# The first transfers of a two-layer decoder trunk: two token tiles on ScalarE's queue, token tiles one piece ahead, a buffer of its own for the fourth unit of weights

## Chip, cores and metric

One core of one Trainium2 chip. The metric is device time in microseconds (us) of one execution, the median of three runs. Engines are called by what they do: TensorE (PE, with PEld for its weight loads) multiplies matrices, VectorE (DVE) and ScalarE (ACT) work elementwise, GpSimd (POOL) does small jobs, and SyncE (SP) issues most transfers from memory. The issuing queues are written SPq and ACTq. The data itself is moved by 16 DMA engines.

## What is computed

Two layers of a causal decoder on 256 tokens of width 2048, in float32. Layer 0 mixes tokens by a block-sparse attention (with 256 tokens only its own block counts, so it is plain causal attention of 16 heads of 128), layer 1 by a latent attention with low-rank queries and keys. Each layer ends with a gated channel mixer of width 5632.

```python
def reference(x, attn_norm, ffn_norm, ...):
    pos = jnp.arange(x.shape[1], dtype=jnp.int32)
    for i in range(DEPTH):
        m, j = i % N_MIXERS, i // N_MIXERS
        h = rms_norm(x, attn_norm[i])
        if m == 0:
            y = moba_attention(h, pos, moba_wq[j], moba_wk[j], moba_wv[j],
                               moba_gq[j], moba_gk[j], moba_wo[j])
        elif m == 1:
            y = mla_attention(h, pos, ...)
        ...
        x = x + y
        h = rms_norm(x, ffn_norm[i])
        x = x + conv_glu_ffn(h, ffn_w_gate[i], ffn_w_up[i], ffn_conv_w[i],
                             ffn_conv_b[i], ffn_w_down[i])
    return x
```

## The kernel before

The tokens lie transposed in one tile `xT`: 16 token tiles of 128 features by 256 tokens, 128 KB each, all in on-chip memory for the whole run. All weights pass by once as a stream (`Stream`, L54). The stream is cut into 370 units, mostly of 1 MB, each of mostly four pieces of 128 x 512 numbers (256 KB). A piece is read from its `raw` buffer and split into a high half `whi` (a cast, L104 on ScalarE; piece 0 alone on VectorE, L102) and a low half `wlo` (the rest, L105 on VectorE), so that TensorE can work at reduced width and add three products: high by high, low by high, high by low. The tokens are split the same way into the two halves of `h` (L279 on ScalarE, L284 on VectorE), after scaling by the gain of the norm; the division by the root mean square comes later, on the result.

The program is a list of quanta, one per piece. Nothing is reordered (`manual_schedule`): for each quantum `q` the last loop (L1049) first runs what was planned ahead of it, then splits pieces up to a few beyond `q` (`ws.split`, L1052; one ahead at first, one more for every six quanta, at most four), then the six products of the piece (`tok_major`, L229, for the first 192 pieces), then what was planned beside it. In the first 16 quanta (the queries of the first four heads) token tile `q` is scaled and split right before its piece, so on ScalarE the order is: high half of tile q, then the cast of the next piece.

Three `raw` buffers hold units (`AHEAD_UNITS = 3`). `split` asks for unit `u + 2` when it starts unit `u` (L96, `load` L66), and the load waits until the unit that had the buffer is split. The first three units, 12 pieces, come as single pieces from `begin` (L75), interleaved with the token tiles: `ends` gives for each piece up to which tile the tokens are asked for right behind it. All of these go out on SP's queue but the very first piece, which is on ScalarE's (L84). The parameters `par` of the norms go first of all. Weight unit 3, the rest of `par`, the rotary tables `tab` and the `gains` follow once the loop runs (`load_constants`, L183, in quantum 9).

The program has eight completion semaphores for these transfers, used in turn: a transfer is issued only when the eighth before it has landed. An issuing queue works strictly in order, so a transfer that waits holds up those behind it.

The attention pool `att` (L165) holds what the attention of layer 0 needs; the latent attention of layer 1 opens another (`att2`) and uses the same helpers. In it are scratch tiles: `junk` (L378) takes the squares that a reduction of VectorE produces on the way to its sums, `ro1` and `ro2` (L430) the two products of the rotation, `kvjunk` (L843) the squares of the latent keys. Each has two buffers, used in turn. `oT` in the same pool is the attention's result, read by TensorE in the output projection (`plan_wo`, L674).

Of the kernel before, what the change touches and what calls it, by code (L numbers as in the profile page):

```python
# [10 lines left out]
F32 = mybir.dt.float32  # L11
# [6 lines left out]
P = 128  # L18
# [24 lines left out]
AHEAD_UNITS = 3  # L43
# [10 lines left out]
class Stream:  # L54
# [17 lines left out]
            self.raw[u] = t  # L72
            self.loaded += 1

    def begin(self, load_x):  # L75

        ends = (2, 2, 3, 4, 6, 6, 8, 8, 10, 10, 13, 16)
        load_x(0, 1)
        at = 1
        for u in range(AHEAD_UNITS):  # L80
            src, k, n = self.units[u]
            self.raw[u] = t = self.raw_pool.tile([P, 4 * 512], F32, name="raw")
            for i in range(k):
                queue = self.nc.scalar if u == i == 0 else self.nc.sync  # L84
                queue.dma_start(t[:, i * n : (i + 1) * n], src[:, i * n : (i + 1) * n])
                end = ends[u * k + i]
                if end > at:
                    load_x(at, end)
                    at = end
        self.loaded = AHEAD_UNITS  # L90

    def split(self, upto):
        while self.split_to < min(upto, len(self.pieces)):
            i = self.split_to
            u, j, n = self.pieces[i]
            self.load(u + AHEAD_UNITS)  # L96
            w = self.raw[u][:, j * n : (j + 1) * n]
            b, c = self.starts(u, j)
            hi = self.part_pool.tile([P, 512 + ROOM], F32R, name="whi")[:, b : b + 512]
            lo = self.part_pool.tile([P, 512 + ROOM], F32R, name="wlo")[:, c : c + 512]  # L100
            if i == 0:
                self.nc.vector.tensor_copy(hi[:, :n], w)  # L102
            else:
                self.nc.scalar.copy(hi[:, :n], w)  # L104
            self.nc.vector.tensor_tensor(  # L105
                lo[:, :n], w, hi[:, :n].bitcast(F32), op=ALU.subtract
            )
            self.parts[i] = (hi, lo, n)
            self.split_to += 1
# [6 lines left out]
def trunk(ctx: ExitStack, tc: tile.TileContext, a, out):  # L116
    nc = tc.nc
# [43 lines left out]
    ws = Stream(nc, raw_pool, part_pool, units, starts)  # L161
# [3 lines left out]
    att_pool = att.enter_context(tc.tile_pool(name="att", bufs=2))  # L165
    xT = keep.tile([P, KD, S], F32, name="xT")
# [9 lines left out]
    warm = const.tile([P, 1], F32, name="warm")  # L176
    nc.scalar.activation(warm, ones, AF.Square)
    nc.sync.dma_start(par[:, :C_CW], a["par"][:, :C_CW])
    ws.begin(lambda j0, j1: nc.sync.dma_start(xT[:, j0:j1, :], a["xT"][:, j0:j1, :]))
    tab = const.tile([P, T_END], F32, name="tab")  # L180
    gains = const.tile([P, G_END], F32, name="gains")

# [170 lines left out]
    class Heads:  # L353
# [21 lines left out]

        def squares(self, t):
            for i in range(self.n):
                junk = att_pool.tile([P, P], F32, name="junk", bufs=2)  # L378
                nc.vector.tensor_tensor_reduce(  # L379
                    out=junk[:, : self.dh], in0=self.x[:, t, i], in1=self.x[:, t, i], scale=1.0,  # L380
                    scalar=0.0, op0=ALU.mult, op1=ALU.add, accum_out=self.ss[:, t, i : i + 1],
                )
# [34 lines left out]
        def rotate(self, t, stages=(0, 1)):  # L417
            if not self.rot:
                return
            n, rot = self.n, self.rot  # L420
            hf = rot // 2
            tb, C, Sn = self.tabs
            ct = tb[:, C + t * rot : C + (t + 1) * rot]
            st = tb[:, Sn + t * rot : Sn + (t + 1) * rot]
            x = self.x[:, t]
            def over(s):
                return s[:, None, :].to_broadcast([P, n, s.shape[1]])

            def part(name):
                r = att_pool.tile([P, 16 * 32], F32, name=name, bufs=2)  # L430
                return r[:, : n * rot].rearrange("p (n r) -> p n r", n=n)

            if 0 in stages:
                t1, t2 = self.rot_parts = part("ro1"), part("ro2")
                nc.vector.tensor_tensor(t1, x[:, :, :rot], over(ct), op=ALU.mult)
                nc.vector.tensor_tensor(t2[:, :, :hf], x[:, :, hf:rot], over(st[:, :hf]), op=ALU.mult)
            if 1 in stages:
                t1, t2 = self.rot_parts
                nc.vector.tensor_tensor(t2[:, :, hf:], x[:, :, :hf], over(st[:, hf:]), op=ALU.mult)
                nc.vector.tensor_tensor(x[:, :, :rot], t1, t2, op=ALU.add)  # L440
# [398 lines left out]
    def kva_stats():  # L839
        ss = small.tile([P, NT, 2], F32, name="kvss")  # L840
        for t in range(NT):
            for k, (lo, hi) in enumerate(((0, 512), (512, 576))):
                junk = att_pool.tile([P, 512], F32, name="kvjunk", tag="ro1", bufs=2)  # L843
                nc.vector.tensor_tensor_reduce(
                    out=junk[:, : hi - lo], in0=env["ckv"][:, t, lo:hi], in1=env["ckv"][:, t, lo:hi],
                    scale=1.0 / (hi - lo), scalar=0.0, op0=ALU.mult, op1=ALU.add,
                    accum_out=ss[:, t, k : k + 1],
                )
        ms = small.tile([P, NT * 2], F32, name="kvms")
        nc.vector.tensor_scalar(ms, ss.rearrange("p t k -> p (t k)"), EPS, None, op0=ALU.add)  # L850
        env["kvr"] = small.tile([P, NT * 2], F32, name="kvr")
        nc.gpsimd.tensor_tensor(env["kvr"], ms, mhalf[:, : NT * 2], op=ALU.pow)
# [144 lines left out]

    at(q, open_room)
    at(q, kva_stats)
    at(q + 3, kva_scale)  # L1000
    at(q + 7, kva_rotate)
# [166 lines left out]
```

## Time and profile before

| | us |
|---|---|
| runs shown: median (lowest, highest) | 2099.79 (2099.7, 2100.92) |
| profiled execution: its own time | 2099.88 |
| its span, first to last instruction | 2098.0 |
| TensorE busy in the span | 2089.0 |
| VectorE busy | 1405.3 |
| ScalarE busy | 1138.3 |
| bytes moved | 391.83 MB |

The profile is of one execution. Times inside it count from the start of its span. A row of a timeline gives the start, the length, the engine, the line of the kernel, the operation and its tiles (written from what is read), and in brackets the idle time before it and what ended that. A row of a transfer gives the tile, the queue and the median time from issue to landing. Products follow each other more closely than their lengths say: they are pipelined, so the distance of two starts is the measure of their rate.

### The profile page before, as it was taken

What the parts mean: (1) busy time and instruction counts of PE and PEld (TensorE: products, weight loads), DVE (VectorE), ACT (ScalarE), POOL (GpSimd) and SP (SyncE); (2) the same over time, 40 slices, a digit from 0 to 9 for tenths busy, and PEclk for the clock granted to TensorE, in tenths of its full rate; (3) what the DMA queues carried; (4) which work ended last, traced back from release to release, by engine and by line L of the source; (5) the groups of instructions that cost most, each with busy time, mean ns of one, the idle gap of its engine ahead of it and who ended that gap; (6) DMA issues with size and microseconds to landing.
All of it is one profiled execution on the core that took longest, in us unless ns stands there. A gap on an engine that the chain in (4) does not pass through costs nothing.

```text
span 2098.0 us, 42200 instructions
## 1 busy us (share of the span) xinstructions
PE 2089.0 (100%) x16716; PEld 2014.2 (96%) x16716; DVE 1405.3 (67%) x3072; ACT 1138.3 (54%) x2238; POOL 45.6 (2%) x37
## 2 busy tenths in 40 slices
PE   9999999999999999999999999999999999999999
PEld 7888889999999999999999889999999999999999
DVE  6776776776666766655556786766766667655554
ACT  6555555655555555545555675655555555544443
POOL 0000000000000000000000110000000000000000
PEclk9999999999999999999999999999999999999999
DMA  7444445555555555555554533555555555555553
GB/s 272 161 170 173 170 171 185 194 188 198 195 190 200 191 191 201 194 190 198 194 191 159 175 139 108 195 181 201 187 196 199 187 199 195 189 205 209 193 207 131
DMA packets 59382, 391.83 MB, mean 187 GB/s; under 512 B 6960, under 2 KB 10032, under 8 KB 13232
## 3 DMA queue, kind: packets, MB, share of 16 engines
q1 hardware_dynamic: 59040, 388.87, 52.3%
q8 instruction: 131, 2.15, 0.4%
q14 instruction: 67, 0.55, 0.1%
q10 hardware_dynamic: 144, 0.26, 0.0%
HBM read 387.01 MB, written 2.10 MB: 185 GB/s over the span
## 4 chain that ended last, share of the span: by engine, by line
PE 96%; DVE 2%; POOL 0%; ACT 0%; issue 0%; DMA 0%; SPq 0%; ACTq 0%; DVEq 0%; POOLq 0%
PE acc L261 26%; PE acc L263 26%; PE acc L262 26%; PE acc L235 15%; PE tp L449 1%; DVE wlo L105 1%; PE sc L489 0%; PE sc L486 0%; PE tp L521 0%; POOL hr L392 0%; DVE junk L379 0%; PE sc L546 0%; DVE qk L405 0%; DMA xT<-in_xT 0%; PE sc L465 0%
## 5 line engine op out<-in xcount | busy, mean ns | idle before, releaser
L105 DVE TENSOR_TENSOR wlo<-raw,whi 128x512 fp32r<-128x512 f32 (+1 forms) x1480 | 1000.1, 684 | 399.0 <-ACT whi L104 396.0
L104 ACT CAST whi<-raw 128x512 fp32r<-128x512 f32 (+1 forms) x1479 | 871.6, 614 | 459.6 <-PE acc L262 212.3
L261 PE MATMUL acc<-h,whi 128*128 128x256 f32 x2880 | 796.1, 276 | 0.0
L263 PE MATMUL acc<-h,wlo 128*128 128x256 f32 x2880 | 795.9, 276 | 0.0
L262 PE MATMUL acc<-h,whi 128*128 128x256 f32 x2880 | 795.8, 276 | 0.0
L261 PEld LDWEIGHTS acc<-h,whi 128*128 128x128 f32 x2880 | 540.9, 188 | 0.0
L263 PEld LDWEIGHTS acc<-h,wlo 128*128 128x128 f32 x2880 | 540.9, 188 | 0.0
L262 PEld LDWEIGHTS acc<-h,whi 128*128 128x128 f32 x2880 | 540.9, 188 | 0.0
L262 PE MATMUL acc<-a,whi 128*128 128x256 f32 x1408 | 389.1, 276 | 0.0
L263 PE MATMUL acc<-a,wlo 128*128 128x256 f32 x1408 | 389.0, 276 | 0.0
L261 PE MATMUL acc<-a,whi 128*128 128x256 f32 x1408 | 389.0, 276 | 0.0
L235 PE MATMUL acc<-whi,h 128*128 128x512 f32 (+1 forms) x896 | 274.6, 381 | 0.0
L263 PEld LDWEIGHTS acc<-a,wlo 128*128 128x128 f32 x1408 | 264.4, 188 | 0.0
L262 PEld LDWEIGHTS acc<-a,whi 128*128 128x128 f32 x1408 | 264.4, 188 | 0.0
L261 PEld LDWEIGHTS acc<-a,whi 128*128 128x128 f32 x1408 | 264.4, 188 | 0.0
L235 PEld LDWEIGHTS acc<-whi,h 128*128 128x128 f32 x896 | 165.0, 188 | 30.0 <-ACT whi L104 0.7
L235 PE MATMUL acc<-wlo,h 128*128 128x512 f32 (+1 forms) x448 | 170.4, 381 | 2.1 <-DVE wlo L105 2.0
L261 PE MATMUL acc<-oT,whi 128*128 128x256 f32 x512 | 144.9, 283 | 0.0
L263 PE MATMUL acc<-oT,wlo 128*128 128x256 f32 x512 | 141.9, 277 | 0.0
L262 PE MATMUL acc<-oT,whi 128*128 128x256 f32 x512 | 141.7, 277 | 0.0
L740 DVE TENSOR_TENSOR g<-acc,rstd_b 128x256 f32<-128x256 f32 x88 | 37.5, 426 | 125.7 <-PE acc L263 122.7
L747 ACT ACTIVATE c<-g,par 128x256 f32<-128x256 f32 x88 | 53.1, 603 | 108.1 <-DVE g L740 108.1
(160 smaller groups left out, 1603.8 us busy)
## 6 DMA issues: line engine op xcount, KB each, us to landing
raw<-in_ffn_gu SPq DMA_DIRECT2D x176, 1024.0 KB, 4.8
raw<-in_ffn_down SPq DMA_DIRECT2D x88, 1024.0 KB, 4.8
raw<-in_moba_wk SPq DMA_DIRECT2D x16, 1024.0 KB, 4.9
raw<-in_moba_wv SPq DMA_DIRECT2D x16, 1024.0 KB, 4.8
raw<-in_moba_wo SPq DMA_DIRECT2D x16, 1024.0 KB, 4.8
raw<-in_mla_wo SPq DMA_DIRECT2D x16, 1024.0 KB, 4.8
raw<-in_moba_wq SPq DMA_DIRECT2D x13, 1024.0 KB, 4.9
raw<-in_mla_wkv_a SPq DMA_DIRECT2D x8, 576.0 KB, 3.7
```

The lines of the kernel that those rows point to most:

```text
L104: self.nc.scalar.copy(hi[:, :n], w)
L105: self.nc.vector.tensor_tensor(lo[:, :n], w, hi[:, :n].bitcast(F32), op=ALU.subtract)
L235: mm(state["acc"][t][:, :n], src[:, kt, c : c + P], (t_lo if part == 1 else t_hi)[:, :n], start=kt == 0 and part == 0, stop=kt == k_last a ...
L261: mm(o, w_hi, src[:, kt, :S], start=first and k == 0, stop=False, skip_group_check=True)
L262: mm(o, w_hi, src[:, kt, S:], start=False, stop=False, skip_group_check=True)
L263: mm(o, w_lo, src[:, kt, :S], start=False, stop=kt == k_last, skip_group_check=True)
L449: nc.tensor.transpose(tp[:, (i * NT + t) * P : (i * NT + t + 1) * P], flat[:, t, c : c + P], ident)
L740: nc.vector.tensor_tensor(self.g[:, 2:], self.gate["acc"][:, :S], self.norm.rstd_b, op=ALU.mult)
L747: nc.scalar.activation(self.c, self.g[:, 2:], AF.Identity, bias=par[:, cb : cb + 1], scale=self.cw(2))
```

## The change

The first transfers are asked for in another order, on two queues, and one buffer is added.

- Behind the first weight piece ScalarE's queue now also asks for token tiles 1 and 2, as one transfer of 256 KB.
- `ends` is new: piece 2 is followed by tile 3, piece 3 by tile 4, and so on singly to tile 7 behind piece 6; then tiles come in pairs, 8 and 9 behind piece 7 up to 14 and 15 behind piece 10. Each tile is asked for before the piece of its number. Before, tile 1 came behind piece 0, tile 2 behind piece 2, tile 3 behind piece 3, then pairs (4 and 5 behind piece 4, and so on) and last two triples.
- Unit 3 gets a buffer named `fourth` of 8 KB per partition in the attention pool and is asked for at the end of `begin`; `split` then asks for unit `u + 3` up to unit 3, which places unit 4 at the start of unit 1, unit 5 at that of unit 2 and unit 6 at that of unit 3. From then on the three `raw` buffers are used as before.
- The scratch tiles `junk`, `ro1`, `ro2` and `kvjunk` have one buffer instead of two.

The work of TensorE, VectorE and ScalarE and its order are the same; ScalarE's queue has one more transfer to issue.

```diff
-    def begin(self, load_x):
-
-        ends = (2, 2, 3, 4, 6, 6, 8, 8, 10, 10, 13, 16)
-        load_x(0, 1)
-        at = 1
+    def begin(self, load_x, fourth):
+
+        sync, act = self.nc.sync, self.nc.scalar
+        ends = (1, 3, 4, 5, 6, 7, 8, 10, 12, 14, 16, 16)
+        load_x(sync, 0, 1)
+        at = 3
         for u in range(AHEAD_UNITS):
             src, k, n = self.units[u]
             self.raw[u] = t = self.raw_pool.tile([P, 4 * 512], F32, name="raw")
             for i in range(k):
-                queue = self.nc.scalar if u == i == 0 else self.nc.sync
+                queue = act if u == i == 0 else sync
                 queue.dma_start(t[:, i * n : (i + 1) * n], src[:, i * n : (i + 1) * n])
+                if u == i == 0:
+                    load_x(act, 1, 3)
                 end = ends[u * k + i]
                 if end > at:
-                    load_x(at, end)
+                    load_x(sync, at, end)
                     at = end
-        self.loaded = AHEAD_UNITS
+        self.raw[AHEAD_UNITS] = fourth
+        sync.dma_start(fourth, self.units[AHEAD_UNITS][0])
+        self.loaded = AHEAD_UNITS + 1
...
-            self.load(u + AHEAD_UNITS)
+            self.load(u + AHEAD_UNITS + (u <= AHEAD_UNITS))
...
-    ws.begin(lambda j0, j1: nc.sync.dma_start(xT[:, j0:j1, :], a["xT"][:, j0:j1, :]))
+    ws.begin(
+        lambda queue, j0, j1: queue.dma_start(xT[:, j0:j1, :], a["xT"][:, j0:j1, :]),
+        att_pool.tile([P, 4 * 512], F32, name="fourth", bufs=1),
+    )
...
-                junk = att_pool.tile([P, P], F32, name="junk", bufs=2)
+                junk = att_pool.tile([P, P], F32, name="junk", bufs=1)
...
-                r = att_pool.tile([P, 16 * 32], F32, name=name, bufs=2)
+                r = att_pool.tile([P, 16 * 32], F32, name=name, bufs=1)
...
-                junk = att_pool.tile([P, 512], F32, name="kvjunk", tag="ro1", bufs=2)
+                junk = att_pool.tile([P, 512], F32, name="kvjunk", tag="ro1", bufs=1)
```

## The prediction

> **What bounds the kernel now.** I read the page first: its span, the busy shares, and the engines of the chain that ended last.
>
> ```profile
> span 2098.0 us, 42200 instructions
> PE 2089.0 (100%) x16716; PEld 2014.2 (96%) x16716; DVE 1405.3 (67%) x3072; ACT 1138.3 (54%) x2238; POOL 45.6 (2%) x37
> PE 96%; DVE 2%; POOL 0%; ACT 0%; issue 0%; DMA 0%; SPq 0%; ACTq 0%; DVEq 0%; POOLq 0%
> ```
>
> TensorE is busy all the time and carries 96% of the chain, and the change touches none of its products. What it can move are the few microseconds at the start in which TensorE has to wait for data. So I next read the chain of waits in the first 14 us (columns: start, length, what).
>
> ```profile
> 4.73 5.04 DMA xT<-in_xT
> 9.79 0.51 ACT h L279
> 10.30 0.52 ACT whi L104
> 10.85 0.70 DVE wlo L105
> 11.59 2.62 PE acc L235 x10
> ```
>
> The fourth token tile (index 3) lands 5.04 us after its issue; then its scaled copy, the high half of weight piece 3 and the low half follow one after the other (0.51 + 0.52 + 0.70 us), and TensorE goes on at 11.59. How much was lost by then, and whether it is the last loss, is read from the timeline of TensorE's products.
>
> ```profile
> 5.33 0.93 PE L235 MATMUL acc<-whi,h 128*128 128x512 f32 x2
> ...
> 14.50 0.39 PE L235 MATMUL acc<-wlo,h 128*128 128x512 f32 x1
> ...
> 22.67 0.39 PE L235 MATMUL acc<-wlo,h 128*128 128x512 f32 x1
> ...
> 23.35 0.39 PE L235 MATMUL acc<-wlo,h 128*128 128x512 f32 x1
> ...
> 27.25 0.39 PE L235 MATMUL acc<-wlo,h 128*128 128x512 f32 x1
> ```
>
> A piece has six products, two of them with the low half, so a low-half product comes every third product. From 14.50 (piece 5, first) to 22.67 (piece 11, first) are 12 such steps in 8.17 us: 0.681 us a step, 1.36 a piece, 0.227 a product, without a gap. The row of 14.50 is the 32nd product; with no wait after 5.33 it would have stood at 5.33 + 31 x 0.227 = 12.37, so 2.13 us are lost up to there. From 23.35 to 27.25 are five steps, 3.41 us by the same rate, but 3.90 pass: another 0.5 us is lost at pieces 12 and 13, after a stretch without any loss. What is late there:
>
> ```profile
> 22.59 0.62 ACT L104 CAST whi<-raw 128x512 fp32r<-128x512 f32 x1 [2.43 <-DMA raw<-in_moba_wq]
> 23.12 0.51 ACT L279 ACTIVATE h<-xT,par 128x256 fp32r<-128x256 f32 x1
> 23.25 0.69 DVE L105 TENSOR_TENSOR wlo<-raw,whi 128x512 fp32r<-128x512 f32 x1 [2.38 <-ACT whi L104]
> 23.86 0.48 DVE L284 SCALAR_TENSOR_TENSOR h<-xT,par,h 128x256 fp32r<-128x256 f32 x1
> 24.39 0.74 PE L235 MATMUL acc<-whi,h 128*128 128x512 f32 x2
> ```
>
> ScalarE sat 2.43 us until weight unit 3 (the fourth megabyte) landed; its token tile 12 is queued behind that cast, VectorE's low half of the tile behind both, and TensorE waits until 24.39. Everything before has waited for this already: a stream that reaches piece 12 earlier only stands there longer. **So the landing of unit 3 at about 22.5 us sets the stream now**, and the change is worth what it moves that landing.
>
> **Unit 3: issue or supply.** Its issue on the SP queue, its time to landing, and the one long issue of the start:
>
> ```profile
> 2.59 1.15 SPq L85
> 14.67 0.33 SPq L71 DMA_DIRECT2D raw<-in_moba_wq  x1
> raw<-in_moba_wq SPq DMA_DIRECT2D x1, 1024.0 KB, 7.8
> ```
>
> It was issued at 14.67 and took 7.8 us. The stretches say why (columns: stretch, length, busy of the five engines, clock, share of the DMA engines, GB/s):
>
> ```profile
> 2.75:5.00 2.25, 2.25 (x6) 0.73 (x5) 0.61 (x2) 0.23 (x1) 0.00 (x0) 1.00 0.97 309
> 5.00:6.75 1.75, 1.75 (x7) 1.25 (x6) 1.33 (x4) 1.30 (x3) 0.00 (x0) 1.00 0.75 218
> 6.75:9.50 2.75, 2.51 (x9) 1.24 (x8) 1.84 (x3) 1.02 (x2) 0.00 (x0) 1.00 0.97 312
> 9.50:12.00 2.50, 2.22 (x8) 1.42 (x9) 1.43 (x4) 1.81 (x4) 0.00 (x0) 1.00 0.93 268
> 12.00:15.00 3.00, 3.00 (x15) 2.33 (x14) 2.51 (x6) 2.32 (x6) 0.00 (x0) 1.00 1.02 375
> 15.00:19.00 4.00, 4.00 (x19) 3.28 (x18) 4.00 (x8) 3.75 (x8) 0.00 (x0) 1.00 1.06 398
> 19.00:22.50 3.50, 3.50 (x17) 2.88 (x17) 1.77 (x4) 1.03 (x2) 0.00 (x0) 1.00 1.03 432
> ```
>
> From 2.75 us on the DMA engines are full but for one dip, and unit 3 stands behind all that was asked for before. In both kernels that is the same: 37 KB of parameters, 16 tiles of 128 KB, 12 pieces of 256 KB, 5,157 KB, then its own 1,024.
>
> **The change part by part.**
>
> *Tiles 1 and 2 from ScalarE's queue as one transfer.*
>
> ```profile
> 0.87 0.38 ACTq L85 DMA_DIRECT2D raw<-in_moba_wq  x1
> ```
>
> ScalarE's second issue stands right behind this first one and ahead of all its copies, which wait for that data anyway, so it delays nothing of ScalarE. SP loses one such issue, some 0.4 us, ahead of pieces 1 and 2, and where piece 2's issue took 1.15 us there now stands tile 3, with 384 KB more already asked for. That can fill the dip: share 0.75 over 1.75 us is 0.25 x 1.75 = 0.44 us of supply. Bounds: 0 (the dip is not a lack of requests, or only on engines that are ahead anyway) to 0.44. I take the upper end, since the dip begins 1.3 us after that issue, 2.59 + 1.15 = 3.74, had ended. Piece 1 gets later, as tile 1 now comes with tile 2: 128 KB at 218 to 309 GB/s are 0.4 to 0.6 us. That is paid from the 2.13 us already lost: the wait at piece 3 was longer.
>
> *Tiles one piece ahead.* Tile 3, and each later one, lands before its piece, so the scaled copy is done when the piece comes: 0.51 us leave the chain shown. With the bytes up to tile 3 and piece 3 the same in both orders, they are complete at
>
> ```profile
> xT<-in_xT SPq DMA_DIRECT2D x1, 128.0 KB, 5.0
> ```
>
> 4.73 + 5.0 = 9.7 us, the low half at 9.7 + 0.62 + 0.69 = 11.0 instead of 11.55. Pieces 3 to 11 gain about half a microsecond; it is all absorbed at piece 12, so it counts nothing. Were unit 3 not late, it would count 0.5.
>
> *Single tiles for 3 to 7, pairs from 8 on.* Six single tiles instead of four: 2 x 128 KB more in the smaller rows. If all the difference between 312 GB/s (a third single tiles) and 375 (none) came from them, that is 3.21 - 2.67 = 0.54 us per MB of mixture, 1.6 per MB of single tiles, 0.42 us for 0.262 MB. Bounds 0 to 0.42; I take the middle, 0.2, since the stretch from 9.50 without single tiles was no faster.
>
> *Unit 3 in its own buffer, and the loads behind it.* It needs no free buffer now. In the built program every DMA waits for the landing of the eighth before it: unit 3 waits for tiles 8 and 9 instead of piece 7, some 250 KB later, and is issued at about 15.4 instead of 14.67. With seven transfers of 256 KB ahead of it (1.8 MB, over 4 us at 398 to 432 GB/s) this stays covered; without that cover it would cost the 0.7. Units 4 and 5 now go out ahead of the constants. Unit 5 was awaited by ScalarE but not by TensorE, which had its pieces ahead, and the constants are needed long after they land:
>
> ```profile
> 32.40 1.14 ACT L104 CAST whi<-raw 128x512 fp32r<-128x512 f32 x2 [2.87 <-DMA raw<-in_moba_wk]
> 20.03 0.33 SPq L191 DMA_DIRECT2D gains<-in_mla_g_kr  x1
> 58.31 0.88 DVE L405 SCALAR_TENSOR_TENSOR qk<-qk,hr,gains 128x128 f32<-128x128 f32 x3 [0.93 <-POOL hr L392]
> ```
>
> Both nothing. From unit 6 on the loop asks for the same unit at the same piece as before.
>
> *One buffer for junk, ro1, ro2, kvjunk.* Only VectorE writes and reads them, in its own order; the built program has 26 more waits of VectorE on itself (24 at line 379). The third square of a group has had that wait all along, the second not:
>
> ```profile
> 53.11 0.28 DVE L379 CUSTOM_DVE_ANT_0 junk<-qk 128x128 f32<-128x128 f32 x1
> 53.31 0.29 DVE L379 CUSTOM_DVE_ANT_0 junk<-qk 128x128 f32<-128x128 f32 x1
> 53.53 0.29 DVE L379 CUSTOM_DVE_ANT_0 junk<-qk 128x128 f32<-128x128 f32 x1
> ```
>
> The step to the second is 0.20, to the third 0.22: 26 x 0.02 = 0.5 us of VectorE at most, over stages where it is 67% busy. Zero. The larger pool moves the attention tiles, oT by 8 KB; products that read oT at two other addresses (one per layer) run as the rest do:
>
> ```profile
> L262 PE MATMUL acc<-oT,whi x512: 275/276/285, 300.1 to 1375.0; 128*128 128x256 f32 x171
> L262 PE MATMUL acc<-h,whi 128*128 128x256 f32 x2880 | 795.8, 276 | 0.0
> ```
>
> **Sum.** Unit 3 lands 0.44 - 0.2 = 0.24 us earlier, say 0.2. Against the profiled execution (2099.88 us around a span of 2098.0) that gives 2099.68; the runs' median, 2099.79, lies 0.09 below it, so **2099.6 us**. Own range: 0.44 gained with no price for small tiles, 2099.3, to 0.42 lost with nothing gained, 2100.2. Changes of under 0.2%, 4.2 us, are what a measurement of this kernel can't tell from none.
>
> The Trainium skill speaks against the 0.44: "DMA: Bandwidth & Descriptors", section "Issuing engines are not separate DMA queues", has it that transfers issued from several engines run on the same 16 DMA engines and interleave, and that only the issuer's own time is saved. By it the term is zero and the time 2100.0; the dip to 0.75 right after the 1.15 us issue is what the trace has against it.
>
> **Rivals.**
>
> *No net effect: the transfers are hidden anyway, 2099.8 to 2100.2.* The dip may lie on DMA engines that are ahead, while the slowest one, which sets each landing, never lacked work. For it: the dip lies at 5 us and the landing at 22.5, with full engines between. Against it: filling 0.44 us anywhere before moves all that follows. Say 2099.9.
>
> *More than the dip: 2098.6.* If the 268 GB/s of 9.50 to 12.00 also come from the order of requests and rise to the 375 of the next stretch, 2.5 x (1 - 268/375) = 0.7 us more; with the 0.44, about 1.2 us. The half microsecond at piece 12 disappears, and the order of tiles pays beyond it. The most that can be gained is all that was lost, 2.13 + 0.5: 2097.2.
>
> *Slower: the later request shows, 2100.9.* Tiles 8 and 9 before:
>
> ```profile
> 9.79 0.49 SPq L179 DMA_DIRECT2D xT<-in_xT  x1
> xT<-in_xT SPq DMA_DIRECT2D x1, 256.0 KB, 6.1
> ```
>
> If they land at 9.79 + 6.1 = 15.9 again, and unit 3 takes its 7.8 us from an issue behind that, its landing moves from 22.5 to 23.7 and TensorE stands 1.2 us longer at piece 12; with 0.1 gained before, 2100.9. It decides once the data ahead is gone before the request reaches the DMA engines. Against it: over 4 us of data are ahead.
>
> *Slower by over 4.2 us:* only a wait in the attention stages could do it, 0.16 us on each of the 26 new waits and all on the path; the rows of line 379 show 0.02.
>
> **How the numbers follow.** Forecast 55%, no net effect 22%, more than the dip 11%, slower by the request 10%, slower by more 2%. The range takes most of the third and fourth case, and the runs' own spread of 1 us: 2098.2 to 2101.1. Faster by over 0.2% would need more than the 2.6 us ever lost: 0.02. Slower 0.03 and the same 0.95.
>
> **What would show it.** Right: a DMA share over 0.9 from 5 to 6.75 us; the low half of piece 3 at about 11.0; ScalarE's wait for unit 3 still there, ending at about 22.3; the rows of line 379 0.21 apart; later stages unmoved. Wrong: no wait for unit 3 at all (the supply was mis-sized), that wait ending after 23 (the request), or the first product clearly after 5.33 and never made up.

## The result, and the profile after

The changed kernel takes 2111.74 us (median of 5 runs, 2110.75 to 2112.11), the kernel before 2099.77 (5 runs, 2099.62 to 2100.92): ratio 1.0054, 95% interval 1.0044 to 1.0065. The forecast was 2099.6, no measurable change; the change costs about 12 us. The profiled execution of the changed kernel took 2110.75 us around a span of 2108.9.

The page of the changed kernel: span, busy time of the engines, and the engines of the chain that ended last.

```profile
span 2108.9 us, 42205 instructions
PE 2090.1 (99%) x16716; PEld 2013.8 (95%) x16716; DVE 1415.6 (67%) x3072; ACT 1138.6 (54%) x2238; POOL 45.5 (2%) x37
PE 91%; DVE 5%; ACT 1%; issue 1%; POOL 1%; DMA 1%; SPq 0%; ACTq 0%; POOLq 0%; DVEq 0%
```

TensorE is as busy as before to 1.1 us, in a span that is 10.9 us longer: it waits more. VectorE's share of the chain rose from 2% to 5%. Where it waits is read from stretches of the run, first of the kernel before, then of the changed one (columns: stretch, length, busy of the five engines, clock, share of the DMA engines, GB/s).

```profile
50.00:100.00 50.00, 48.86 (x237) 40.28 (x236) 38.17 (x130) 28.67 (x63) 4.68 (x3) 1.00 0.44 154
100.00:200.00 100.00, 99.64 (x486) 83.01 (x486) 74.08 (x225) 55.49 (x124) 5.96 (x3) 1.00 0.48 169
200.00:300.00 100.00, 100.00 (x482) 83.18 (x481) 72.19 (x224) 55.01 (x118) 5.83 (x3) 1.00 0.50 178
300.00:1100.00 800.00, 800.00 (x7056) 799.89 (x7055) 529.81 (x973) 429.52 (x807) 1.07 (x1) 1.00 0.54 193
1100.00:1250.00 150.00, 147.84 (x930) 131.81 (x929) 111.30 (x405) 96.10 (x227) 20.98 (x13) 1.00 0.45 156
```

```profile
50.00:100.00 50.00, 47.79 (x228) 38.79 (x228) 37.85 (x125) 27.18 (x60) 4.81 (x3) 1.00 0.42 152
100.00:200.00 100.00, 97.64 (x478) 81.22 (x477) 74.09 (x225) 54.50 (x124) 5.96 (x3) 1.00 0.46 165
200.00:300.00 100.00, 98.11 (x467) 81.14 (x466) 72.40 (x212) 54.50 (x116) 5.83 (x3) 1.00 0.49 173
300.00:1100.00 800.00, 800.00 (x7034) 799.04 (x7033) 530.06 (x981) 429.17 (x809) 1.08 (x1) 1.00 0.54 193
1100.00:1250.00 150.00, 144.44 (x931) 129.67 (x930) 110.04 (x371) 92.27 (x214) 18.91 (x12) 1.00 0.44 152
```

The loss lies in the two attention stages: 1.1, 2.0, 1.9 and 3.4 us of TensorE's busy time are missing in these stretches (layer 1's attention runs past 1250 us, and so does its loss); in the 800 us between them nothing. The starts of the 16,080 weight products in the two traces place it more closely. The difference is +0.13 us at piece 16, grows by eight steps of 0.72 to 0.74 us between 62 and 289 us, one for each group of query or key heads of layer 0, stands at 6.0 until layer 1's attention, and rises there to 10.9.

**What a step consists of.** The squares of one group in the changed kernel's timeline of VectorE (start, length, instruction):

```profile
53.24 0.29 DVE L387 CUSTOM_DVE_ANT_0 junk<-qk 128x128 f32<-128x128 f32 x1
53.45 0.08 DVE L387 DVE_READ_ACCUMULATOR2_ANT ss<- 128x1 f32 x1
53.56 0.29 DVE L387 CUSTOM_DVE_ANT_0 junk<-qk 128x128 f32<-128x128 f32 x1
53.78 0.08 DVE L387 DVE_READ_ACCUMULATOR2_ANT ss<- 128x1 f32 x1
53.90 0.29 DVE L387 CUSTOM_DVE_ANT_0 junk<-qk 128x128 f32<-128x128 f32 x1
...
54.45 0.69 DVE L110 TENSOR_TENSOR wlo<-raw,whi 128x512 fp32r<-128x512 f32 x1
55.05 0.28 DVE L387 CUSTOM_DVE_ANT_0 junk<-qk 128x128 f32<-128x128 f32 x1
```

From square to square it is 0.32 to 0.34 us; in the prediction's rows of the same place before it was 0.20 to 0.22. The squares themselves last 0.29 in both. Before, a square began together with the read of the accumulator of the one ahead; now it begins 0.03 us after that read (0.08 long) has ended. Two rows of the kernel before:

```profile
53.31 0.08 DVE L379 DVE_READ_ACCUMULATOR2_ANT ss<- 128x1 f32 x1
53.31 0.29 DVE L379 CUSTOM_DVE_ANT_0 junk<-qk 128x128 f32<-128x128 f32 x1
```

The groups of lines say the same for all 128 squares of the query and key heads: busy time of the line, mean ns of one, and idle time just before them, before and after.

```profile
L379 DVE CUSTOM_DVE_ANT_0 junk<-qk 128x128 f32<-128x128 f32 x128 | 29.6, 289 | 0.0
```

```profile
L387 DVE CUSTOM_DVE_ANT_0 junk<-qk 128x128 f32<-128x128 f32 x128 | 37.1, 290 | 3.3
```

The same squares cover 7.5 us more of VectorE's time, since they no longer overlap with their neighbours, and 3.3 us are idle besides: 10.8. (That TensorE's loss is about as large is a coincidence: VectorE has 32 more squares, of the rotary queries, and TensorE does not lose all of it.) A square with a low half between it and the last one (55.05, 0.60 after that low half began, 0.61 before) pays nothing, so three of every four pay 0.12.

**How it reaches TensorE.** VectorE's later rows of this group in the changed kernel, and TensorE's wait behind them:

```profile
59.16 1.14 DVE L413 SCALAR_TENSOR_TENSOR qk<-qk,hr,gains 128x128 f32<-128x128 f32 x4 [0.93 <-POOL hr L400]
...
63.72 2.49 DVE L110 TENSOR_TENSOR wlo<-raw,whi 128x512 fp32r<-128x512 f32 x4
```

```profile
62.91 0.61 PE L243 MATMUL acc<-whi,h 128*128 128x512 f32 x2
64.46 0.50 PE L243 MATMUL acc<-wlo,h 128*128 128x512 f32 x1 [0.93 <-DVE wlo L110]
```

Squares, mean, GpSimd's power, scaling and rotation follow one another, and the low half that TensorE needs next is queued behind them. The scaling began at 58.31 before, now at 59.16. The same product of TensorE in the kernel before:

```profile
62.66 0.61 PE L235 MATMUL acc<-whi,h 128*128 128x512 f32 x2
63.60 0.50 PE L235 MATMUL acc<-wlo,h 128*128 128x512 f32 x1 [0.33 <-DVE wlo L105]
```

It waited there already. So in this group there was no slack: 63.60 became 64.46, 0.86 later, 0.13 of it from the start and 0.73, about 6 x 0.12, from this group. The waits of TensorE's weight loads for a low half, between 40 and 310 us and between 1100 and 1260 us (us in total, times, longest), are 4.4 and 2.2 before:

```profile
PEld acc L235 <- DVE wlo L105: 4.4, 8, 1.2
...
PEld acc L235 <- DVE wlo L105: 2.2, 5, 1.2
```

and 10.5 and 6.2 after:

```profile
PEld acc L243 <- DVE wlo L110: 10.5, 10, 1.5
...
PEld acc L243 <- DVE wlo L110: 6.2, 8, 1.6
```

**The start after.** The stretches of the prediction again, in the changed kernel:

```profile
2.75:5.00 2.25, 2.25 (x7) 0.71 (x5) 0.41 (x1) 0.00 (x0) 0.00 (x0) 1.00 0.95 284
5.00:6.75 1.75, 1.33 (x6) 0.98 (x6) 1.59 (x4) 1.46 (x3) 0.00 (x0) 1.00 1.05 382
6.75:9.50 2.75, 2.53 (x12) 1.75 (x11) 2.54 (x5) 2.75 (x7) 0.00 (x0) 1.00 1.07 353
9.50:12.00 2.50, 2.50 (x13) 2.07 (x12) 1.88 (x5) 1.59 (x5) 0.00 (x0) 1.00 0.94 306
12.00:15.00 3.00, 3.00 (x15) 2.49 (x14) 2.45 (x5) 1.64 (x4) 0.00 (x0) 1.00 0.93 240
15.00:19.00 4.00, 4.00 (x18) 2.79 (x17) 1.84 (x4) 2.16 (x5) 0.00 (x0) 1.00 1.04 383
19.00:22.50 3.50, 3.50 (x16) 2.74 (x16) 2.52 (x5) 1.97 (x4) 0.00 (x0) 1.00 1.04 437
```

The dip is filled (382 GB/s for 218), and given back from 12 to 15 us (240 for 375). Each stretch's GB/s times its length, added up from 2.75 to 22.50 us, is 6.82 MB now and 6.83 MB before. Unit 3 lands no earlier, and TensorE still stands at piece 12:

```profile
22.70 0.62 ACT L109 CAST whi<-fourth 128x512 fp32r<-128x512 f32 x1 [1.44 <-DMA fourth<-in_moba_wq]
23.78 0.51 PE L243 MATMUL acc<-whi,h 128*128 128x512 f32 x1 [0.46 <-ACT h L287]
```

### The profile page after: what moved, and what is told of

It reads as the page before. It is cut to its first block, busy times and chain, and to the rows that moved or that the text cites. A ratio compares the mean times of both kernels' runs of the same rounds, so it can differ in the third digit from the quotient of the medians.

```text
span 2108.9 us, 42205 instructions
## 1 busy us (share of the span) xinstructions
PE 2090.1 (99%) x16716; PEld 2013.8 (95%) x16716; DVE 1415.6 (67%) x3072; ACT 1138.6 (54%) x2238; POOL 45.5 (2%) x37
## 4 chain that ended last, share of the span: by engine, by line
PE 91%; DVE 5%; ACT 1%; issue 1%; POOL 1%; DMA 1%; SPq 0%; ACTq 0%; POOLq 0%; DVEq 0%
PE acc L271 26%; PE acc L269 26%; PE acc L270 26%; PE acc L243 10%; DVE wlo L110 2%; DVE junk L387 1%; POOL hr L400 1%; DVE qk L413 1%; PE tp L457 1%; ACT whi L109 0%; PE tp L529 0%; PE sc L497 0%; PE sc L494 0%; ACT qk L382 0%; DMA fourth<-in_moba_wq 0%
```

## The experiments

Theory: with one buffer for `junk`, each square must wait for the one directly before it, 0.12 us each, which VectorE passes on to TensorE. Rivals: the scratch of the rotation, the moved attention tiles, or the new first transfers. "Stream" below is the start of a product of the profiled run minus that of the same product in the kernel before, at four places; the last column is the median of the runs.

| kernel | piece 16 | 310 us | 1100 us | after layer 1's attention | time, us |
|---|---|---|---|---|---|
| changed kernel | +0.13 | +6.0 | +6.0 | +10.9 | 2111.74 |
| e1_junk_one | -0.27 | +5.5 | +5.5 | +9.8 | 2110.17 |
| e2_rotation_one | +2.33 | +2.4 | +2.4 | +2.8 | 2100.54 |
| e3_after_two | +1.03 | +1.05 | +1.05 | +1.0 | 2100.95 |
| e4_two_single | +0.19 | +0.2 | +0.2 | +0.2 | 2099.59 |
| e5_half | +0.25 | +3.2 | +3.2 | +5.2 | 2105.11 |
| e6_junk_four | +0.03 | +0.1 | +0.1 | +0.1 | 2099.94 |
| e7_spaced | -0.12 | -2.6 | -2.6 | -1.9 | 2098.45 |
| e8_spaced_one | +0.11 | -0.8 | -0.8 | +5.9 | 2104.70 |
| e9_spaced_late | +0.17 | -3.2 | -3.2 | -3.2 | 2096.71 |
| e10_late_two_single | -1.15 | -4.5 | -4.5 | -4.5 | 2096.08 |

### One buffer for junk alone

```diff
-                junk = att_pool.tile([P, P], F32, name="junk", bufs=2)
+                junk = att_pool.tile([P, P], F32, name="junk", bufs=1)
```

> The kernel before with one edit: junk, the scratch output of the squares, has one buffer instead of two. Theory (each square now waits for the end of the square directly before it): squares that follow each other step by 0.33 us instead of 0.21; six such steps in each group of eight squares, 0.73 us on TensorE's stream at each of the 16 groups, about 11 us in all: 2110.8 us. Rival, the moved attention tiles or the single buffers of the rotation cost it: 2099.8, steps of 0.21. Rival, the new first transfers cost it: 2099.8.

Measured: 2110.17 us, ratio to the kernel before 1.0047 (1.0032 to 1.0062), before 2100.08. From piece 16 on the stream loses 5.8 us in layer 0 and 4.3 in layer 1, and its squares stand 0.33 apart. One number of the diff makes 10.1 of the 12 us, at the places and by the steps of the changed kernel. The total came near the expected 11, but not by the expected parts. In layer 0 each of the eight groups costs 0.70 to 0.74, as expected. In layer 1 the waits come to some 9.1 us of VectorE (eight groups of six, and 28 of the rotary queries, which the expectation left out), and 4.3 of them reach TensorE: by where the steps stand, the first rotary queries (1.7) and the first two groups (1.4) pay in full, and all that follows adds 1.2.

### One buffer for the rotation's scratch alone

```diff
-                r = att_pool.tile([P, 16 * 32], F32, name=name, bufs=2)
+                r = att_pool.tile([P, 16 * 32], F32, name=name, bufs=1)
...
-                junk = att_pool.tile([P, 512], F32, name="kvjunk", tag="ro1", bufs=2)
+                junk = att_pool.tile([P, 512], F32, name="kvjunk", tag="ro1", bufs=1)
```

> The kernel before with one edit: ro1, ro2 and kvjunk have one buffer each instead of two; junk keeps two. Theory of the squares: 2099.8, within 0.3. Rival, the rotation's scratch is part of the loss, two writes for each of the groups that wait for the sum before: up to 0.12 us for each of two parts of 16 groups, 2 to 4 us: 2102 to 2104.

Measured: 2100.54, ratio 1.0003 (0.9994 to 1.0013). The profiled run lost 2.3 us in the first 30 us, which the edit does not touch (its first product came at 6.10 us instead of 5.33), and then 0.4 at one place near 1173 us: the four squares of `kvjunk`, which now wait for each other three times, 3 x 0.12. The rotation itself pays nothing: by the time `ro1` is written again, the sum that read it is followed by a low half and four scalings.

### The changed kernel with two buffers

```diff
-                junk = att_pool.tile([P, P], F32, name="junk", bufs=1)
+                junk = att_pool.tile([P, P], F32, name="junk", bufs=2)
...
-                r = att_pool.tile([P, 16 * 32], F32, name=name, bufs=1)
+                r = att_pool.tile([P, n * rot], F32, name=name, bufs=2)
...
-                junk = att_pool.tile([P, 512], F32, name="kvjunk", tag="ro1", bufs=1)
+                junk = att_pool.tile([P, 512], F32, name="kvjunk", tag="ro1", bufs=2)
```

> The changed kernel with two buffers again for junk, ro1, ro2 and kvjunk; room for them comes from cutting ro1 and ro2 to the numbers they use in layer 0 (128 instead of 512). First transfers, load order, the buffer of unit 3 and the moved attention tiles stay. Theory of the squares: the 11 us are gone; what is left is the start, +0.13 us by the stream: 2099.9, steps of 0.21. Rival, moved tiles or new transfers: 2110 to 2112.

Measured: 2100.95, ratio 1.0003 (0.9994 to 1.0012). All of the stream's +1.0 stands at piece 16; from there to the end it moves by less than 0.1. The attention tiles still lie behind the new buffer of unit 3, as in the changed kernel, so their moved place costs nothing that the stream shows, and the new transfers cost or gain what the start shows, no more. Together with e1_junk_one this settles the cause.

### Unit 3 in quarters

```diff
-        sync.dma_start(fourth, self.units[AHEAD_UNITS][0])
+        src, k, n = self.units[AHEAD_UNITS]
+        for i in range(k):
+            sync.dma_start(fourth[:, i * n : (i + 1) * n], src[:, i * n : (i + 1) * n])
```

> The kernel of e3_after_two with weight unit 3 loaded as four transfers of 256 KB instead of one of 1024 KB. If the landing of the whole unit sets the stream at piece 12: the first quarter lands some 1.5 us before the last, TensorE does not wait there, and the gain of the earlier pieces (0.9 to 1.1 us at pieces 4 and 9) is kept: 2098.9 us. If the supply of bytes itself sets it: 2099.9, the wait only moves from piece 12 to pieces 13 to 15.

Measured: 2099.59, ratio 0.9996 (0.9986 to 1.0005): within the spread. The start of this run:

```profile
18.00 0.50 PE L245 MATMUL acc<-whi,h 128*128 128x512 f32 x1 [0.24 <-ACT h L289]
...
21.26 0.62 ACT L111 CAST whi<-raw 128x512 fp32r<-128x512 f32 x1 [0.30 <-DMA raw<-in_moba_wq]
...
22.20 0.60 ACT L111 CAST whi<-fourth 128x512 fp32r<-128x512 f32 x1
```

The wait for unit 3 is gone: its first quarter is cast at 22.20 without one, 0.50 us before the same cast of the changed kernel (22.70) and 1.43 before that of e3_after_two (23.63), whose third piece had already begun 0.60 later than the changed kernel's (9.57 against 8.97). But TensorE now waits at 18.00, at the first quarter of unit 2, and ScalarE for the landing of that unit's quarters up to the last of them (21.26). So the landing of unit 3 as a whole was a limit, and right behind it lies the supply of bytes; half of each theory holds, and 2098.9 was not reached.

### Half the dose

```diff
-                junk = att_pool.tile([P, P], F32, name="junk", bufs=2)
+                junk = att_pool.tile([P, P], F32, name=("junk", "junk1")[t], bufs=1 + t)
```

> The kernel before; the squares of the first 128 tokens (t = 0) write to a junk of one buffer, those of the second (t = 1) to a junk of their own with two. Theory (0.12 us for each square behind another one that writes the same buffer, passed on in full to TensorE): three waits a group instead of six, half of the 10.1 us of the kernel with one buffer for all, 2105.1 us, the four squares of t = 0 0.33 apart, those of t = 1 0.21. Rival, part of the delay is taken up by slack before it reaches TensorE: the first half costs less than 4, 2102 to 2104. Rival, the groups have a threshold that the first three waits already cross: over 6, 2106 to 2109.

Measured: 2105.11, ratio 1.0023 (1.0014 to 1.0033), 4.94 above the kernel before (2100.17): half of e1_junk_one's 10.1. One kernel shows both steps, 0.33 with one buffer and 0.21 with two:

```profile
53.36 0.29 DVE L379 CUSTOM_DVE_ANT_0 junk<-qk 128x128 f32<-128x128 f32 x1
53.57 0.08 DVE L379 DVE_READ_ACCUMULATOR2_ANT ss<- 128x1 f32 x1
53.69 0.29 DVE L379 CUSTOM_DVE_ANT_0 junk<-qk 128x128 f32<-128x128 f32 x1
...
55.18 0.28 DVE L379 CUSTOM_DVE_ANT_0 junk<-qk 128x128 f32<-128x128 f32 x1
55.39 0.08 DVE L379 DVE_READ_ACCUMULATOR2_ANT ss<- 128x1 f32 x1
55.39 0.29 DVE L379 CUSTOM_DVE_ANT_0 junk<-qk 128x128 f32<-128x128 f32 x1
```

In layer 0 each group costs 0.35 to 0.38, three times 0.12: no slack takes up the first three waits there, and there is no threshold. Layer 1 loses 2.0 us instead of 4.3, so there, too, about half.

### Four buffers

```diff
-                junk = att_pool.tile([P, P], F32, name="junk", bufs=2)
+                junk = att_pool.tile([P, P], F32, name="junk", bufs=4)
```

> The kernel before with four buffers for junk instead of two. If a write to the buffer of two squares before costs nothing, because that square is done by then: steps of 0.21 and the time of before, 2099.8 within 1. Rival, two buffers already pay part of the wait: steps under 0.20 and up to 3 us faster, 2097.

Measured once: 2099.94, steps of 0.21. Two buffers pay nothing; the whole price lies between one and two. The traces record which instruction waits for a semaphore, the counter that another one raises when it is done, and say why. Of the 96 squares that directly follow another, 75 carry a wait on VectorE's own count with two buffers and 33 with four, and with and without it they step by 0.20 to 0.23. In the changed kernel all 96 carry one, now on the square directly ahead, and all step by 0.32 to 0.34.

### Room behind the squares

```diff
         for t in range(NT):
-            at(q + step * (5 + t), hs.scaled, t)
-            at(q + step * (5 + t), hs.rotate, t)
+            at(q + step * (5 + 2 * t), hs.scaled, t)
+            at(q + step * (6 + 2 * t), hs.rotate, t)
```

e8_spaced_one makes this edit and that of e1_junk_one.

> The kernel before with the second half of each head group's work spread: scaling of t = 0 five pieces after the group's last product, its rotation six, scaling of t = 1 seven, its rotation eight (before: five, five, six, six). Nothing is added or removed. If the low halves queued behind scaling and rotation on VectorE are what TensorE waits for at the groups (4.4 us of waits between 40 and 310 us, 2.2 between 1100 and 1260): those waits go, 4 to 6 us faster, 2094 to 2096. Rival, TensorE waits there for something that stays in place (GpSimd's power, the weights): 2099.8 within 0.5.

> The spread order of e7_spaced and one buffer for junk. If the waits between squares cost TensorE time only because VectorE is already late behind them in each group: with room made there most of the 10.1 us is hidden, at most 3 us above e7_spaced. Rival, a wait of VectorE on itself costs TensorE its full length wherever it stands: 10 us above e7_spaced.

Measured: 2098.45, ratio 0.9991 (0.9981 to 1.0000), and, with one buffer, 2104.70, ratio 1.0022 (1.0013 to 1.0031). The gain is 1.7 us, not 4 to 6, with an interval that reaches none, and the price of the one buffer 6.2, not 3. Layer 0 bears the theory out: TensorE no longer waits for a low half there at all. What it waits for between 40 and 310 us with two buffers, and then with one:

```profile
PE tp L449 <- DVE qk L440: 0.6, 1, 0.6
```

```profile
PE tp L449 <- DVE qk L440: 1.7, 3, 1.4
```

The wait went one place on, to transposes of the rotated tile (at their weight loads it is 1.0 and 2.8 us). From 30 us to 310 the one buffer costs 1.6 us in this order (from -2.6 - (-0.1) to -0.8 - 0.1) instead of 5.8. In layer 1 no room was made (its groups have no rotation, and the second scaling came a piece later): the one buffer costs 6.0 there, for 4.3 in the old order, and the spreading alone 0.7. So in layer 0 the same 0.12 us a square is mostly hidden once VectorE has room, 1.6 us of 5.8 being left; in layer 1, which got none, 6.0 of some 9.1 us reach TensorE.

### Spread in layer 0 alone, and that with the mended start

Against the kernel before; of the head groups only those of layer 0 have `hs.rot`, a rotation. In the first groups of layer 0 (`g == 0`) the transposes and scores also come one piece later. e10_late_two_single makes the same edit in the kernel of e4_two_single.

```diff
-            at(q + step * (5 + t), hs.scaled, t)
-            at(q + step * (5 + t), hs.rotate, t)
+            a = 2 * t if hs.rot else t
+            at(q + step * (5 + a), hs.scaled, t)
+            at(q + step * (6 + a), hs.rotate, t)
...
-                           queries_out if kind == "q" else keys_out, 1)
+                           queries_out if kind == "q" else keys_out, 2 if g == 0 else 1)
...
-            q0 = q_k + (13 if g else 21) + (2 * i if g == 3 else 3 * i)
+            q0 = q_k + (13 if g else 22) + (2 * i if g == 3 else 3 * i)
```

> The kernel before with the spread order in layer 0 alone, and in its first head groups the transposes and scores one piece later. In e7_spaced one wait of 1.0 us on TensorE moved to a transpose behind the rotated tile, and layer 1 lost 0.7 us on its stream. If both were costs of spreading too far: they go, 3.3 us faster than before on the stream, 2096.7 to 2097.2. Rival, the wait only moves one place further again: 2098.4, as e7_spaced.

> The order of e9_spaced_late in the kernel of e4_two_single (two buffers, the new first transfers, unit 3 in quarters). If the start of e4_two_single is worth the 0.5 us by which its runs were faster: 0.5 below e9_spaced_late. Rival, that was chance, or the start is no faster than the one of before: the same as e9_spaced_late or up to 0.9 above it, as with e3_after_two.

Measured: 2096.71, ratio 0.9986 (0.9977 to 0.9996), and 2096.08, ratio 0.9981 (0.9972 to 0.9991), before 2099.78. Both beat the kernel before; the second also holds the new first transfers and is the best of all kernels run. The 0.6 between the two is less than the intervals can tell. The page of the second:

```profile
span 2093.2 us, 42210 instructions
PE 99%; DVE 1%; DMA 0%; issue 0%; ACT 0%; POOL 0%; SPq 0%; POOLq 0%; ACTq 0%
```

TensorE's share of the chain rises from 96% to 99%. Of the 38 us that VectorE had in the chain before, 25.0 lay between 40 and 310 us, and there it has none now; the 12.1 us of layer 1's attention are still there.

## Why the prediction was wrong

**The step that failed** is "*One buffer for junk, ro1, ro2, kvjunk*", in its sentence "The step to the second is 0.20, to the third 0.22: 26 x 0.02 = 0.5 us of VectorE at most". Three things were wrong in it.

- *The row was no measure of the new wait.* With two buffers the third square waits for the first, which has ended by then; that wait is met each time (75 such squares, in steps of 0.21 but for one of 0.23). With one buffer the second waits for the first, which is still running. I compared two waits by their existence and not by which instruction they wait for.
- *The count was wrong.* The traces bear out the 26 more waiting instructions, but these are not 26 more stalls: the waits that were there all along moved one square nearer. Those that pay are 6 in each of 16 groups of query and key heads, 96, and 7 in each of the 4 rows of eight squares of the rotary queries, 28 more. At 0.12 each these 124 are 14.9 us of VectorE, of which 10.1 reach TensorE.
- *"67% busy" was taken for cover.* That is VectorE's share of the whole run; in the four stretches of the attention stages shown above it is 72 to 76%, and within a group of layer 0 VectorE had no cover, as TensorE's 0.33 us wait at 63.60 shows. The prediction counted TensorE's losses at the start alone. The view that shows the others is that of the weight loads' waits for a low half from 40 to 310 us (4.4 us in total).

The price could be read in the trace of before. Its timeline of one rotation:

```profile
59.69 0.22 DVE L436 TENSOR_TENSOR ro<-qk,tab 128x64 f32<-128x64 f32 x1
59.83 0.22 DVE L439 TENSOR_TENSOR ro<-qk,tab 128x64 f32<-128x64 f32 x1
60.08 0.29 DVE L440 TENSOR_TENSOR qk<-ro,ro 128x128 f32<-128x128 f32 x1
```

The second product doesn't need the first and follows after 0.14 us; the sum needs both and follows the second after 0.25: 0.11 us more for the same length, when an instruction waits for the one directly before it. With that row the 96 waits of the head groups alone come to 96 x 0.11 = 10.6 us, and the time to 2110. That this meets the measured 10.1 is in part luck: layer 0 pays its 48 waits in full (5.8 us), layer 1 only 4.3 us of 76 x 0.12 = 9.1.

The Trainium skill, "VectorE: DVE Perf Modes", section "The DRAIN you can't avoid", would have misled here too: it reports that chained VectorE copies take the same time with a semaphore after each as with one after the last, so that a semaphore adds nothing. The squares agree for a wait that is already met and differ for one on the instruction directly ahead: 0.33 against 0.21 us a step, in one kernel (e5_half).

**Slower by over 4.2 us** was the case that came true, and it had 2%. Its place was right (a wait in the attention stages, most of it on the path), its price of 0.16 us near the measured 0.12, its count of 26 far below the 124; it was held down by the same wrong row. Of the prediction's own signs two failed with it: the rows of the squares stand 0.33 apart and not 0.21, and the later stages moved.

**What was right.** TensorE bounds the kernel, and it does so still. The dip was filled (share 1.05 for 0.75), as *Tiles 1 and 2 from ScalarE's queue* had it; which part of the new order filled it was not tried. *Tiles one piece ahead* came true and by more than said: the low half of piece 3 began at 8.96 us and ended 0.69 later, at 9.65 (11.0 forecast, 11.54 before), and the gain, 1.15 us at piece 4 and 1.23 at most, was gone at piece 12 (0.03), as said. ScalarE's wait for unit 3 is still there. *The moved attention tiles* cost nothing (e3_after_two), and neither did the later constants.

**What was off in the start.** Unit 3's cast began at 22.70, not at about 22.3: the 0.44 of the dip came back as a slow stretch from 12 to 15 us, and of the rivals "no net effect" fits this part. The Trainium skill, "DMA: Bandwidth & Descriptors", section "Issuing engines are not separate DMA queues", has it that a second issuing engine saves only the issuer's time; by the sum of bytes up to 22.50 us (6.82 and 6.83 MB) the trace agrees. What slowed the stretch from 12 to 15 was not tried. Unit 3 was issued at 14.51, not 15.4, so the later request that was priced at nothing did not come about. A term of 0.2 us could not be tested here at all: the stream at piece 16 differs by up to 2.6 us between e1_junk_one and e2_rotation_one, whose starts are the same.

*ro1, ro2 and kvjunk* were priced at nothing and cost 0.4 us, at the four squares of `kvjunk`.

Squares (10.1) and `kvjunk` (0.4) account for 10.5 of the 10.8 us that the changed kernel's stream loses after piece 16; the other 0.3 lie mostly in layer 1 and were not followed up. The runs' median is 1.0 above the profiled run, less than the starts differ among themselves.

## What to carry to other kernels

A second buffer for a scratch tile that nobody reads is not waste when consecutive instructions of one engine write it: with one buffer each waits for the end of the last, where otherwise they overlap. When a change cuts a buffer count, ask for each wait which instruction it now waits for, how far back that is, and price it by a pair of neighbouring rows that do depend on each other. Before calling an engine's added time hidden, look for waits on that engine in the same stage, however small: where the bound engine already waited for it, in layer 0 here, every tenth of a microsecond went through, and in layer 1 about half.

## What the runs showed of the hardware that was not expected

- In the rows here a VectorE instruction that waits for the one directly before it starts 0.03 us after that one's last part has ended; one that doesn't starts some 0.08 us before that end. For the 128x128 square with its accumulator read this is 0.33 against 0.21 us a step, over half as much again; for the 128x64 squares of the rotary queries 0.26 to 0.27 against 0.14 to 0.15: the same 0.12.
- A wait that is already met costs nothing here (75 squares before, 33 with four buffers, in steps of 0.21 to 0.23). Nor are two writes to one place needed for the price: the rotation's sum waits for the product ahead of it and writes another tile, and it, too, starts 0.03 us after that product's end. Squares that write one place without a wait were not tried.
- An instruction between hides it: the square behind a low half of 0.69 us pays nothing.
- With the same instructions up to then, the first product of the eight profiled kernels with the old start stood between 5.10 and 6.10 us, and the stream at piece 16 between -0.27 and +2.33 us of the kernel before.
